# Latent attention: probabilities copied within SBUF ahead of rounded 32-bit transposes, with SyncE in source order

## The chip, the cores and the metric

The kernel runs on one core of a Trainium2 chip. The metric is the time of one execution on the device in microseconds (us). A core has TensorE (PE; its weight loads are shown as PEld), VectorE (DVE), ScalarE (ACT), GpSimd (POOL) and SyncE (SP), which here only issues transfers (DMAs). ScalarE, VectorE and TensorE meet in PSUM, the matmuls' output memory; all else lies in SBUF, the on-chip memory, or in DRAM. A time is given as the median of several runs; the profile comes from one profiled execution.

## What is computed

One decoder block with two attention mixers in parallel, for 1024 tokens of width 1024 in float32: sliding-window attention (A) and multi-head latent attention (B), gated and summed, then a gated feed-forward part. The change is in B, which has 8 heads, keys of 64 + 32 numbers and values of 64, and is causal:

```python
def one_block(args):
    qn, qr, n = args
    s = (einsum('bqhd,bkhd->bhqk', qn, k_nope) + einsum('bqhr,bkr->bhqk', qr, k_rope)) * scale
    qpos = n * BLOCK + jnp.arange(BLOCK)
    causal = kpos[None, :] <= qpos[:, None]
    s = jnp.where(causal[None, None], s, -jnp.inf)
    p = jax.nn.softmax(s, axis=-1).astype(v.dtype)
    return jnp.einsum('bhqk,bkhd->bqhd', p, v)
...
y = sigmoid(g_a) * (o_a @ w_o_swa) + sigmoid(g_b) * (o_b @ w_o_mla)
x = x + y @ w_out
h = rmsnorm(x)
x = x + (silu(h @ w_gate) * (h @ w_up)) @ w_down
```

The queries are swept in blocks of 128. Block n has n + 1 blocks of keys.

## The kernel before

**Numbers in two halves.** The matmuls take a 32-bit type that is rounded (`F32R`, "rounded 32-bit"). To keep accuracy an operand is split into a rounded part and the rest: `split` casts on ScalarE (L163) and subtracts on VectorE (L166), and `mm3` adds three products (L172 to L174). A tile of type `F32R` must be written as such; the kernel gets round this for the windowed attention by copying a float32 tile by DMA into an `F32R` tile, whose bits are then taken as they are (`norm`, the `move` entry, L1095, and `sw_pT`, L1008).

**The stage around the change.** After the projections (`prod_q`, `prod_k`, `prod_v`, `prod_rope`) comes a loop over 64 steps t, 8 heads by 8 query blocks. Within a head the blocks are taken in the order 2, 3, 6, 7, 0, 1, 4, 5 (`order`), so a step handles 3, 4, 7, 8, 1, 2, 5 or 6 blocks of keys. `scores(t)` multiplies into a score tile `scb` in PSUM (two buffers); VectorE adds the mask and takes the extreme (L1263); ScalarE takes the exponential with its row sum into `p` in SBUF (L1264); GpSimd inverts the sum (L1265) and scales `p` (L1266). `transposes(t)` turns each 128x128 block of `p` by TensorE (L1280) into PSUM tiles `pTb` of up to four blocks and splits them into `pth` and `ptl`. `pv` multiplies two query blocks by the values (L1302, L1303) three steps later.

In step t the source issues `scores(t + 2)`, then `pv`, the loads of a later head's queries and keys (`load_q`, three transfers of 768 KB in all, in the fifth step of a head; `load_k`, 512 KB, in the seventh), then two of the products of the gated output projection of A as filler (`mix_a`, tile `oA`), then `transposes(t)`. Behind these come transfers and splits for the filler and for the stage that follows: gate tiles (`load_sig`, `sg`), weights (`st.load_to`, `wr`), and `out_sums`, which adds blocks of the output weights in DRAM, by copies that SP issues (two of 1 MB at t = 34, one each at t = 47 and 54) and by accumulating transfers that GpSimd issues (t = 40, 43, 50, 58). `prod_k` for later heads runs in the first steps and stores its result to DRAM (`kn_d`, L1211); `mix_a` stores four of its tiles (`ar_d`, L1364).

**What sets the order.** Until the loop TensorE and SP follow the source by hand. In the loop they do not: a planner orders each engine's instructions by its own estimate of costs, except for those marked to keep their place. Tiles of one pool are given out as they come free: 21 shared slots of 4 KB a partition (`U`) hold `p`, `pth`, `ptl`, `sg`, `wr` and others. A transfer's issue waits on its engine until its data and its slot are ready, and what stands behind it on that engine waits too.

Of the kernel before, what the change touches and what calls it, by code (L numbers as in the profile page):

```python
# [17 lines left out]
P = 128  # L18
# [71 lines left out]
def hybrid_block_kernel(  # L90
# [39 lines left out]
    def psum_phase(name, bufs):  # L130
        if psum:
            psum.pop("cm").close()
        psum["cm"] = ExitStack()
        psum["x"] = psum["cm"].enter_context(tc.tile_pool(name=name, bufs=bufs, space=PSUM))
# [18 lines left out]
    def P1(name, shape=(P, 512), dt=F32):  # L153
        return ps1.tile(list(shape), dt, tag="ps", name=uid(name))
# [6 lines left out]
    def split(hi, lo, src, eng=None):  # L161

        i = nc.scalar.copy(hi, src)  # L163
        if held[0]:
            tc.keep_in_program_order(i)
        (eng or nc.vector).tensor_tensor(lo, src, hi.bitcast(F32), op=ALU.subtract)  # L166
# [15 lines left out]
    def blk(b, n=1):  # L182
        return slice(b * P, (b + n) * P)

    def half(s):
        return slice(512 * s, 512 * s + 512)
# [1014 lines left out]
    def prod_k(j, s):  # L1201
        ps = P1("k")
        mm3(ps, [((wk[0][:, k, blk(j)], wk[1][:, k, blk(j)]), (ckv[k][0][:, half(s)], ckv[k][1][:, half(s)]))
                 for k in range(2)])
        if j == 0:
            for u in range(2):
                split(kT[u][0:64, 0, half(s)], kT[u][0:64, 1, half(s)], ps[64 * u:64 * u + 64])
            return
        t = U("kns", F32R, (P, 2, 512))
        split(t[:, 0], t[:, 1], ps)  # L1210
        nc.sync.dma_start(kn_d[j][:, :, half(s)], t.bitcast(F32))  # L1211

    def prod_v(b):
        ps = P1("v")
        mm3(ps, [((ckv[k][0][:, blk(b)], ckv[k][1][:, blk(b)]), (wv[0][:, k], wv[1][:, k])) for k in range(2)])
        if b % 2 == 0:
            t = V("vM", F32R, (P, 2, NH, P))
            vM.extend([t[:, 0], t[:, 1]])
        split(vM[b][:, :, 0:HD], vM[b][:, :, HD:P], ps.rearrange("p (h d) -> p h d", d=HD))

    def load_k(h):
        nc.sync.dma_start(kT[h % 3][0:64].bitcast(F32), kn_d[h // 2, 64 * (h % 2):64 * (h % 2) + 64])

    def load_q(h):
        if h >= 2:
            qT[h] = V("qT", F32R, (P, 2, S))
            nc.sync.dma_start(qT[h][0:64].bitcast(F32), qn_d[h // 2, 64 * (h % 2):64 * (h % 2) + 64])
        t = qT[h]
        for i in range(2):
            nc.sync.dma_start(t[64 + 16 * i:80 + 16 * i].bitcast(F32), qr_d[i, 16 * h:16 * h + 16])  # L1230
# [11 lines left out]
    def scores(t):  # L1242
        h, n = step(t)
        w = (n + 1) * P
        sc = PX("scb", (P, 1024))
        qh, ql = (qT[h][0:QK, i] for i in range(2))
        kh, kl = (kT[h % 3][0:QK, i] for i in range(2))
        cw = 320 if w == 640 else 512
        for c0 in range(0, w, cw):
            c1 = min(c0 + cw, w)  # L1250
            kc = slice(c0, c1)
            o = slice(c0 // cw * 512, c0 // cw * 512 + c1 - c0)
            nc.tensor.matmul(sc[:, o], qh[:, blk(n)], kh[:, kc], start=True, stop=False)
            nc.tensor.matmul(sc[:, o], qh[:, blk(n)], kl[:, kc], start=False, stop=False)
            nc.tensor.matmul(sc[:, o], ql[:, blk(n)], kh[:, kc], start=False, stop=True)  # L1255
        nm = tiny("nmb")
        p = U("p")
        den = tiny("denb")
        s_, m_, p_ = sc[:, 0:w], mask[:, S - w:], p[:, 0:w]
        if cw == 320:  # L1260
            s_ = sc.rearrange("p (a c) -> p a c", a=2)[:, :, 0:320]
            m_, p_ = (v.rearrange("p (a c) -> p a c", a=2) for v in (m_, p_))
        nc.vector.tensor_tensor_reduce(s_, s_, m_, 1.0, -NEG, op0=ALU.add, op1=ALU.min, accum_out=nm)  # L1263
        nc.scalar.activation(p_, s_, AF.Exp, scale=-1.0, bias=nm, accum_out=den)  # L1264
        nc.gpsimd.tensor_tensor(den, den, neg_one[:, 0:1], op=ALU.pow)  # L1265
        nc.gpsimd.tensor_scalar(p[:, 0:w], p[:, 0:w], den, 0.0, op0=ALU.mult, op1=ALU.add)  # L1266
        live[t] = p

    def transposes(t):
        h, n = step(t)  # L1270
        p = live.pop(t)
        j, odd = divmod(n, 2)
        if not odd:
            pts[(h, j)] = [(U("pth", F32R, (P, 4, 256)), U("ptl", F32R, (P, 4, 256)))
                           for _ in range((2 * j + 5) // 4)]
        for k0 in range(0, n + 1, 4):
            m = min(4, n + 1 - k0)
            pp = P1("pTb", (P, 4, P))
            for i in range(m):
                nc.tensor.transpose(pp[:, i], p[:, blk(k0 + i)], ident)  # L1280
            hi, lo = pts[(h, j)][k0 // 4]
            split(hi[:, 0:m, blk(odd)], lo[:, 0:m, blk(odd)], pp[:, 0:m])

    def pv(h, j):
        tiles = pts.pop((h, j))
# [57 lines left out]
    def mix_a(dc, sh, c0, n, ps=None):  # L1343
        if ps is not None:
            oa_ps[(dc, sh)] = ps
        ps = oa_ps[(dc, sh)]
        if (sh, c0) == (0, 0):
            if dc >= 4:
                ar[dc] = gate[dc]
            elif dc % 2 == 0:  # L1350
                t = V("ar", F32, (P, 2, S))
                ar[dc], ar[dc + 1] = t[:, 0], t[:, 1]
            if dc % 2 == 0:
                wo[dc // 2] = st.get(("oa", dc // 2))
        w = wo[dc // 2]
        mm3(ps, [((w[0][:, c, blk(dc % 2)], w[1][:, c, blk(dc % 2)]), oaT[(c, sh)]) for c in range(c0, c0 + n)],
            c0 == 0, c0 + n == 4)
        if c0 + n == 4:
            nc.vector.scalar_tensor_tensor(ar[dc][:, half(sh)], gate[dc][:, half(sh)], 1.0, oa_ps.pop((dc, sh)),
                                           op0=ALU.add, op1=ALU.mult)  # L1360
            if sh == 1:
                gate.pop(dc)
                if dc >= 4:
                    nc.sync.dma_start(ar_d[dc - 4], ar.pop(dc))  # L1364

    obT = {}

# [41 lines left out]
    prod_q(3, 0)  # L1409
    prod_q(3, 1)  # L1410
    psum_phase("psb", 2)
    prod_v(4)
    scores(0)
    prod_k(1, 0)
# [1 line left out]
    scores(1)  # L1416
    prod_v(5)
    prod_v(6)
    prod_v(7)
    load_k(2)  # L1420
    first = {0: (2, 0), 1: (2, 1), 2: (3, 0), 3: (3, 1)}
    fill = {}
# [4 lines left out]
    w_at = {t: u[0] // 2 for t, u in fill.items() if u[0] % 2 == 0 and u[1:] == (0, 0)}  # L1427
    g_at = {a: fill[b][0] for a, b in zip([3] + slots, slots) if fill[b][1:] == (0, 0)}
    g_at[NT - 3] = 3
    pvq = []  # L1430
    OUT_AT = {34: 0, 40: 1, 43: 2, 47: 3, 50: 4, 54: 5, 58: 6}
    for t in range(NT):
        h, n = divmod(t, NB)
        if t + 2 < NT:
            scores(t + 2)
        while pvq and pvq[0][0] <= t:
            pv(*pvq.pop(0)[1:])
        if n == 4 and h + 2 < NH:
            load_q(h + 2)
        if n == 6 and h + 3 < NH:  # L1440
            load_k(h + 3)
        hh, nn = step(t)
        if nn % 2 == 1:
            pvq.append((t + 3, hh, nn // 2))
        e = t - (NT - 8)
        if e == 6:
            psum_phase("psc", 4)
        if t in first:
            prod_k(*first[t])
        if t in fill:  # L1450
            dc, sh, c0 = fill[t]
            mix_a(dc, sh, c0, 2, P1("oA") if c0 == 0 else None)
        if t == NT - 1:
            mix_a(13 // 2 ^ 4, 13 % 2, 0, 4, PX("oA"))
        transposes(t)
        if t in OUT_AT:
            out_sums(OUT_AT[t])
        held[0] = True
        if t in g_at:
            load_sig(g_at[t])  # L1460
        if t in fill and fill[t][1:] == (0, 0):
            twice_sigmoid(gate[fill[t][0]])
        if t == NT - 1:
            twice_sigmoid(gate[3])
        if t == 3:
            load_oa(0, 1)
            load_oa(1, 1)
        if t < 4 or 6 <= t < 10:
            split_oa(t % 4 // 2 if t < 4 else (t - 6) // 2, t // 6, t % 2)
        if t + 6 in w_at or t == 0:  # L1470
            st.load_to(st.index[("oa", w_at.get(t + 6, 2))])
        if t + 2 in w_at:
            st.conv_to(st.index[("oa", w_at[t + 2])])
        if e == 4:
            load_sigs(DCS[0])
        if -3 <= e < 3:
            split_ob((e + 3) // 2, (e + 3) % 2)
        if e in (2, 6):
            st.load_to(st.index[("ob", 0 if e == 2 else 2)])
        if e == 6:  # L1480
            st.conv_to(st.index[("ob", 0)])
        held[0] = False
    rest = [(i // 2 ^ 4, i % 2) for i in range(14, 16)]
    mix_a(*rest.pop(0), 0, 4, PX("oA"))
    for _, hp, j in pvq:
# [626 lines left out]
```

## Time and profile before

| | |
|---|---|
| median of 3 runs | 1323.54 us (1322.53 to 1324.08) |
| span of the profiled execution | 1323.3 us |
| busy: PE, DVE, ACT, POOL | 99%, 69%, 48%, 42% of the span |
| granted TensorE clock | 0.999 of full speed |
| DMA | 245.12 MB, mean 185 GB/s |
| transposes of the latent attention, first to last start | 386.0 to 553.1 us |

A row of the groups names the line of the code, the engine, the operation, and the tiles as out<-in; then count, and durations in ns. A row of the timeline gives start and duration in us, then the same names, and in brackets the idle time before it with what ended it. A row of the waits says who waited for whom, with the total in us, the times and the longest. A row of the transfers gives the tiles, the issuing queue (SPq, POOLq), the count, the size of one and the median time from issue to landing. Successive matmuls overlap in their records, so their price is the distance of their starts.

### The profile page before, as it was taken

Reading aid. Unit: us, or ns where it says so; the run is one execution under the profiler, and the core shown is the slowest. Engines: PE = TensorE matmul, PEld = TensorE weight load, DVE = VectorE, ACT = ScalarE, POOL = GpSimd, SP = SyncE. Lnnn points to the kernel's source line nnn. Section 1 sums busy time; section 2 is a strip of 40 time slices with the busy share of each in tenths; the row PEclk is TensorE's granted clock in tenths of the full one; section 3 lists DMA queues with packets and bytes.
Section 4 is the critical chain, followed back from the end, with each engine's and each line's share of the span. In section 5 each row is a group of like instructions: output and inputs, shape, how many; then the busy total and the mean of one; then the engine's idle time right before and its main releaser. Section 6 shows DMA issues by size and latency. Waiting matters only on the chain.

```text
span 1323.3 us, 19060 instructions
## 1 busy us (share of the span) xinstructions
PE 1310.9 (99%) x6516; PEld 1103.7 (83%) x6516; DVE 917.0 (69%) x1517; ACT 634.6 (48%) x1282; POOL 559.0 (42%) x619
## 2 busy tenths in 40 slices
PE   9999999999999999999999999999999999999997
PEld 6899888888888889888888888888888888888886
DVE  6868787786767777777779655656666554664863
ACT  7444667665557666755355232323222223644452
POOL 1116545653324556312232465777567631022521
PEclk9999999999999999999999999999999999999999
DMA  9464344456577477898531334655544435996504
GB/s 359 167 195 154 125 162 145 140 184 212 166 241 201 97 223 160 277 322 195 181 122 48 112 130 172 235 195 206 183 181 148 150 112 198 378 376 224 175 17 142
DMA packets 92192, 245.12 MB, mean 185 GB/s; under 512 B 10304, under 2 KB 17984, under 8 KB 90944
## 3 DMA queue, kind: packets, MB, share of 16 engines
q1 hardware_dynamic: 87264, 233.15, 50.9%
q0 software_dynamic: 3392, 8.39, 3.6%
q10 hardware_dynamic: 1440, 2.36, 0.5%
q8 instruction: 52, 0.85, 0.3%
q14 instruction: 44, 0.36, 0.1%
HBM read 161.16 MB, written 78.51 MB: 181 GB/s over the span
## 4 chain that ended last, share of the span: by engine, by line
PE 63%; DVE 2%; issue 1%; POOL 1%; ACT 1%; POOLq 0%; DVEq 0%; ACTq 0%
PE fa L174 6%; PE fa L172 6%; PE fa L173 6%; PE fd L173 5%; PE fd L172 5%; PE fd L174 5%; PE fb L173 5%; PE fb L174 5%; PE fb L172 5%; PE xo L174 2%; PE xo L172 2%; PE xo L173 2%; PE pTb L1280 1%; PE oB L174 1%; PE oB L172 1%
## 5 line engine op out<-in xcount | busy, mean ns | idle before, releaser
L166 DVE TENSOR_TENSOR wl<-wr,wl 128x512 fp32r<-128x512 f32 x150 | 142.5, 973 | 74.7 <-ACT wl L163 74.2
L166 DVE TENSOR_TENSOR lrv<-lr,lrv 128x1024 fp32r<-128x1024 f32 x77 | 105.5, 1401 | 48.2 <-ACT lrv L163 45.6
L163 ACT CAST lrv<-lr 128x1024 fp32r<-128x1024 f32 x77 | 80.2, 1054 | 90.4 <-PE fd L174 56.7
L172 PE MATMUL fd<-lrv 128*128 128x512 f32 x308 | 119.8, 389 | 0.0
L173 PE MATMUL fd<-lrv 128*128 128x512 f32 x308 | 119.8, 389 | 0.0
L174 PE MATMUL fd<-lrv 128*128 128x512 f32 x308 | 119.8, 389 | 0.0
L177 POOL TENSOR_TENSOR wr<-wr,sm 128x512 f32<-128x512 f32 (+1 forms) x38 | 45.5, 1208 | 139.9 <-DVE wl L166 121.7
L163 ACT CAST wl<-wr 128x512 fp32r<-128x512 f32 x150 | 86.7, 621 | 4.8 <-DVE t3l L177 2.8
L166 DVE TENSOR_TENSOR wl<-sm,wl 128x512 fp32r<-128x512 f32 x60 | 50.2, 859 | 42.1 <-ACT wl L163 41.9
L1265 POOL TENSOR_TENSOR denb<-denb,neg_one 128x1 f32<-128x1 f32 x64 | 39.8, 622 | 92.7 <-ACT p L1264 80.7
L172 PEld LDWEIGHTS fd<-lrv 128*128 128x128 f32 x308 | 57.8, 188 | 12.1
L174 PEld LDWEIGHTS fd<-lrv 128*128 128x128 f32 x308 | 57.8, 188 | 12.0
L173 PEld LDWEIGHTS fd<-lrv 128*128 128x128 f32 x308 | 57.8, 188 | 11.9
L1264 ACT ACTIVATE p<-scb,nmb 128x384 f32<-128x384 f32 (+3 forms) x64 | 47.7, 746 | 32.0 <-DVE nmb L1263 23.5
L361 POOL TENSOR_SCALAR ms<-ss 128x1 f32<-128x1 f32 x32 | 8.9, 278 | 125.9 <-ACT xn L1742 47.5
L1263 DVE CUSTOM_DVE_ANT_0 scb<-scb,mask 128x384 f32<-128x384 f32 (+3 forms) x64 | 48.5, 761 | 17.2 <-PE scb L1255 14.6
L1638 ACT ACTIVATE act<-sm 128x512 f32<-128x512 f32 x11 | 7.0, 635 | 102.1 <-DVE sm L180 102.1
L166 DVE TENSOR_TENSOR ptl<-pTb,pth 128x512 fp32r<-128x512 f32 (+2 forms) x96 | 50.0, 550 | 7.9 <-ACT pth L163 7.7
L163 ACT CAST pth<-pTb 128x512 fp32r<-128x512 f32 (+2 forms) x96 | 43.4, 480 | 18.1 <-PE pTb L1280 17.1
L1266 POOL TENSOR_SCALAR p<-p,denb 128x384 f32<-128x384 f32 (+3 forms) x64 | 48.2, 753 | 6.3
L172 PE MATMUL fa<-t1h,wl 128*128 128x512 f32 x120 | 47.1, 392 | 0.4 <-ACT wl L163 0.4
L172 PE MATMUL fb<-t2h,wl 128*128 128x512 f32 x120 | 47.1, 392 | 0.0
(357 smaller groups left out, 4260.7 us busy)
## 6 DMA issues: line engine op xcount, KB each, us to landing
lr<-la_d SPq DMA_DIRECT2D x77, 256.0 KB, 5.4
wr<-in_w_gate_dram SPq DMA_DIRECT2D x22, 512.0 KB, 4.3
wr<-in_w_up_dram SPq DMA_DIRECT2D x22, 512.0 KB, 5.0
la_d<-sd SPq DMA_DIRECT2D x22, 512.0 KB, 5.2
wd<-in_w_down_dram SPq DMA_DIRECT2D x22, 512.0 KB, 6.6
rb_d<-wd SPq DMA_DIRECT2D x22, 512.0 KB, 2.7
lr<-rb_d SPq DMA_DIRECT2D x44, 256.0 KB, 5.4
lr<-in_w_down_dram SPq DMA_DIRECT2D x33, 256.0 KB, 5.4
```

Source lines behind the costliest of these rows:

```text
L163: i = nc.scalar.copy(hi, src)
L166: (eng or nc.vector).tensor_tensor(lo, src, hi.bitcast(F32), op=ALU.subtract)
L172: nc.tensor.matmul(ps, ah, bh, start=first and i == 0, stop=False, skip_group_check=go_on)
L173: nc.tensor.matmul(ps, ah, bl, start=False, stop=False, skip_group_check=go_on)
L174: nc.tensor.matmul(ps, al, bh, start=False, stop=last and i == n - 1, skip_group_check=go_on)
L177: eng.tensor_tensor(out, a, b, op=ALU.subtract)
L361: nc.gpsimd.tensor_scalar(ms, ss, 1.0 / width, EPS, op0=ALU.mult, op1=ALU.add)
L1263: nc.vector.tensor_tensor_reduce(s_, s_, m_, 1.0, -NEG, op0=ALU.add, op1=ALU.min, accum_out=nm)
L1264: nc.scalar.activation(p_, s_, AF.Exp, scale=-1.0, bias=nm, accum_out=den)
L1265: nc.gpsimd.tensor_tensor(den, den, neg_one[:, 0:1], op=ALU.pow)
L1266: nc.gpsimd.tensor_scalar(p[:, 0:w], p[:, 0:w], den, 0.0, op0=ALU.mult, op1=ALU.add)
L1280: nc.tensor.transpose(pp[:, i], p[:, blk(k0 + i)], ident)
```

## The change

It has five parts. (1) `scores` no longer hands `p` to the transposes: `move()` allocates a tile `pr` of rounded type and has SP copy the used columns of `p` into it; one is issued in each step behind `transposes(t)`, and two before the loop, for which `scores(2)` moves ahead of the loop. (2) The transposes read `pr`, with the rounded identity, into a PSUM tile of rounded type, which is read back as float32. (3) In the loop the scores run three steps ahead (`AHEAD = 3`) and not two. (4) The stores of `kn_d` and `ar_d` are put into a list, `later`, and issued by `stores()` once a step, after `scores` and `pv`. (5) From `prod_v(4)` to the end of the loop SP follows the source's order; in it `load_q` and `load_k` come behind the transposes and the copy.

```diff
--- before.py
+++ after.py
@@ -1208,7 +1208,7 @@
             return
         t = U("kns", F32R, (P, 2, 512))
         split(t[:, 0], t[:, 1], ps)
-        nc.sync.dma_start(kn_d[j][:, :, half(s)], t.bitcast(F32))
+        later.append((kn_d[j][:, :, half(s)], t.bitcast(F32)))
 
     def prod_v(b):
         ps = P1("v")
@@ -1264,7 +1264,19 @@
         nc.scalar.activation(p_, s_, AF.Exp, scale=-1.0, bias=nm, accum_out=den)
         nc.gpsimd.tensor_tensor(den, den, neg_one[:, 0:1], op=ALU.pow)
         nc.gpsimd.tensor_scalar(p[:, 0:w], p[:, 0:w], den, 0.0, op0=ALU.mult, op1=ALU.add)
-        live[t] = p
+        moves.append((t, p, w))
+
+    moves = []
+    later = []
+
+    def move():
+        t, p, w = moves.pop(0)
+        live[t] = U("pr", F32R)
+        nc.sync.dma_start(live[t].bitcast(F32)[:, 0:w], p[:, 0:w])
+
+    def stores():
+        while later:
+            nc.sync.dma_start(*later.pop(0))
 
     def transposes(t):
         h, n = step(t)
@@ -1275,11 +1287,11 @@
                            for _ in range((2 * j + 5) // 4)]
         for k0 in range(0, n + 1, 4):
             m = min(4, n + 1 - k0)
-            pp = P1("pTb", (P, 4, P))
+            pp = P1("pTb", (P, 4, P), F32R)
             for i in range(m):
-                nc.tensor.transpose(pp[:, i], p[:, blk(k0 + i)], ident)
+                nc.tensor.transpose(pp[:, i], p[:, blk(k0 + i)], ident_r)
             hi, lo = pts[(h, j)][k0 // 4]
-            split(hi[:, 0:m, blk(odd)], lo[:, 0:m, blk(odd)], pp[:, 0:m])
+            split(hi[:, 0:m, blk(odd)], lo[:, 0:m, blk(odd)], pp.bitcast(F32)[:, 0:m])
 
     def pv(h, j):
         tiles = pts.pop((h, j))
@@ -1361,7 +1373,7 @@
             if sh == 1:
                 gate.pop(dc)
                 if dc >= 4:
-                    nc.sync.dma_start(ar_d[dc - 4], ar.pop(dc))
+                    later.append((ar_d[dc - 4], ar.pop(dc)))
 
     obT = {}
 
@@ -1409,6 +1421,8 @@
     prod_q(3, 0)
     prod_q(3, 1)
     psum_phase("psb", 2)
+    sp_order = tc.manual_schedule(engines={engines.SP})
+    sp_order.__enter__()
     prod_v(4)
     scores(0)
     prod_k(1, 0)
@@ -1416,7 +1430,11 @@
     scores(1)
     prod_v(5)
     prod_v(6)
+    move()
+    stores()
+    scores(2)
     prod_v(7)
+    move()
     load_k(2)
     first = {0: (2, 0), 1: (2, 1), 2: (3, 0), 3: (3, 1)}
     fill = {}
@@ -1427,18 +1445,16 @@
     w_at = {t: u[0] // 2 for t, u in fill.items() if u[0] % 2 == 0 and u[1:] == (0, 0)}
     g_at = {a: fill[b][0] for a, b in zip([3] + slots, slots) if fill[b][1:] == (0, 0)}
     g_at[NT - 3] = 3
+    AHEAD = 3
     pvq = []
     OUT_AT = {34: 0, 40: 1, 43: 2, 47: 3, 50: 4, 54: 5, 58: 6}
     for t in range(NT):
         h, n = divmod(t, NB)
-        if t + 2 < NT:
-            scores(t + 2)
+        if t + AHEAD < NT:
+            scores(t + AHEAD)
         while pvq and pvq[0][0] <= t:
             pv(*pvq.pop(0)[1:])
-        if n == 4 and h + 2 < NH:
-            load_q(h + 2)
-        if n == 6 and h + 3 < NH:
-            load_k(h + 3)
+        stores()
         hh, nn = step(t)
         if nn % 2 == 1:
             pvq.append((t + 3, hh, nn // 2))
@@ -1453,6 +1469,12 @@
         if t == NT - 1:
             mix_a(13 // 2 ^ 4, 13 % 2, 0, 4, PX("oA"))
         transposes(t)
+        if moves:
+            move()
+        if n == 4 and h + 2 < NH:
+            load_q(h + 2)
+        if n == 6 and h + 3 < NH:
+            load_k(h + 3)
         if t in OUT_AT:
             out_sums(OUT_AT[t])
         held[0] = True
@@ -1480,6 +1502,8 @@
         if e == 6:
             st.conv_to(st.index[("ob", 0)])
         held[0] = False
+    stores()
+    sp_order.__exit__(None, None, None)
     rest = [(i // 2 ^ 4, i % 2) for i in range(14, 16)]
     mix_a(*rest.pop(0), 0, 4, PX("oA"))
     for _, hp, j in pvq:
```

## The prediction

> **What bounds the kernel now.** I read the page's totals first, then the busy time of the stage that the change touches (its first and last transposes date it: 386 to 553 us), then what ends the waits there.
>
> ```profile
> span 1323.3 us, 19060 instructions
> PE 1310.9 (99%) x6516; PEld 1103.7 (83%) x6516; DVE 917.0 (69%) x1517; ACT 634.6 (48%) x1282; POOL 559.0 (42%) x619
> ```
>
> ```profile
> 386.00:554.00 168.00, 165.05 (x1059) 144.93 (x1058) 129.60 (x271) 118.90 (x266) 88.64 (x128) 1.00 0.67 182
> 554.00:600.00 46.00, 46.00 (x212) 38.38 (x211) 34.06 (x50) 24.23 (x31) 7.06 (x8) 1.00 0.99 329
> ```
>
> The columns after the window are its length, busy PE, PEld, DVE, ACT and POOL, the granted clock, the DMA engines' share and GB/s. TensorE is busy in 165.05 of the stage's 168 us and in all 46 us behind it, at full clock, so a TensorE microsecond saved here reaches the end if nothing new makes it wait. The next engine, VectorE, is at 77% in the stage. The DMA engines stand at 0.67.
>
> ```profile
> PEld scb L1253 <- ACT p L1264: 1.7, 5, 0.5
> ...
> PEld pTb L1280 <- POOL p L1266: 0.8, 1, 0.8
> ```
>
> These are TensorE's two longest waits for the softmax in the stage, the score products' for a score tile that the exponential still reads and the transposes' for the scaled probabilities: 2.5 us (the columns are total, times, longest).
>
> **The transposes.** The change makes the 288 transposes of the probabilities 32-bit rounded. The form has rows already: the windowed attention transposes such tiles at L1008.
>
> ```profile
> L1280 PEld LDWEIGHTS pTb<-ident_r,p x288: 137/140/145, 385.8 to 553.0; 128*128 128x128 f32 x144
> L1280 PE MATMUL pTb<-ident_r,p x288: 270/272/328, 386.0 to 553.1; 128*128 128x128 f32 x144
> ```
>
> ```profile
> L1008 PEld LDWEIGHTS pT<-ident_r,per x120: 137/139/143, 152.7 to 316.3; 128*128 128x128 f32 x120
> L1008 PE MATMUL pT<-ident_r,per x120: 222/247/253, 152.9 to 316.4; 128*128 128x128 f32 x120
> ```
>
> The durations (272 and 247 ns) overlap from one instruction to the next, so the price is the distance of starts. First the plain form, then the rounded one, both in TensorE's order of time:
>
> ```profile
> 479.00 0.93 PE L1280 MATMUL pTb<-ident_r,p 128*128 128x128 f32 x7
> 479.68 0.36 PE L1253 MATMUL scb<-kT,qT 96*128 96x256 f32 x1
> 479.88 0.28 PE L1254 MATMUL scb<-kT,qT 96*128 96x256 f32 x1
> 480.00 0.28 PE L1255 MATMUL scb<-kT,qT 96*128 96x256 f32 x1
> ```
>
> ```profile
> 175.22 0.80 PE L1008 MATMUL pT<-ident_r,per 128*128 128x128 f32 x8
> 175.85 0.33 PE L948 MATMUL qT<-ident_r,qn 128*128 128x128 f32 x2
> 176.02 0.47 PE L172 MATMUL fb<-t3h,wl 128*128 128x512 f32 x1
> 176.33 0.40 PE L173 MATMUL fb<-t3l,wl 128*128 128x512 f32 x1
> 176.56 0.40 PE L174 MATMUL fb<-t3h,wl 128*128 128x512 f32 x1
> ```
>
> A 256-column product normally takes 0.12 (479.88 to 480.00), so the seven plain transposes hold the array until 479.88 - 0.12 = 479.76: 0.76 us, 0.109 each. In the second list a 512-column product takes 0.23, so the ten rounded ones hold it until 176.10: 0.88 us, 0.088 each; inside the group they stand (175.85 - 175.22)/8 = 0.079 apart, and 176.10 - 176.02 = 0.08 follows the group as a bubble. A group of n therefore costs 0.079n + 0.08 against 0.109n. A head has 36 blocks in eight groups (1 to 8 blocks): 36 x 0.030 - 8 x 0.08 = 0.44 us a head, 3.5 us in eight heads. If neighbouring groups run together, it is 288 x 0.021 = 6.0; with no bubble at all, 288 x 0.030 = 8.6. I take 4.5, between the first two, since the groups here are as mixed as in the row of ten. The evacuations (cast on ScalarE, subtraction on VectorE) keep their shapes and counts.
>
> [...]
>
> **The copy.** In its place comes, for each of the 64 steps, one transfer within SBUF of the tile's used columns (64 KB for each of 1 to 8 blocks). It stands between GpSimd's scaling (L1266) and the transposes, so its latency lies on the path of every step. In exchange the scores are issued three steps ahead and not two. What a step has now:
>
> ```profile
> 435.92 1.12 POOL L1266 TENSOR_SCALAR p<-p,denb 128x1024 f32<-128x1024 f32 x1
> ...
> 437.65 0.37 POOL L1266 TENSOR_SCALAR p<-p,denb 128x128 f32<-128x128 f32 x1
> ...
> 442.96 0.48 POOL L1266 TENSOR_SCALAR p<-p,denb 128x256 f32<-128x256 f32 x1
> ```
>
> ```profile
> 438.38 1.04 PE L1280 MATMUL pTb<-ident_r,p 128*128 128x128 f32 x8
> 441.03 0.30 PE L1280 MATMUL pTb<-ident_r,p 128*128 128x128 f32 x1
> 444.12 0.38 PE L1280 MATMUL pTb<-ident_r,p 128*128 128x128 f32 x2
> ```
>
> From the end of the scaling to the first transpose lie 438.38 - 437.04 = 1.3 us (8 blocks), 3.0 (1 block) and 0.7 (2 blocks), 1.7 on the mean. A step lasts (553.1 - 386.0)/63 = 2.65 us, by the first and last starts of the transposes quoted above. One step more ahead makes the room 4.3 us on the mean, 4.0 for the 512 KB tile, 3.3 for the 128 KB one. The copy's price:
>
> ```profile
> per<-pe SPq DMA_DIRECT2D x14, 512.0 KB, 3.2
> ...
> lat_d<-lat SPq DMA_DIRECT2D x8, 128.0 KB, 1.7
> ```
>
> The windowed attention's copy of 512 KB within SBUF lands 3.2 us after issue; the nearest small transfer, to DRAM, takes 1.7. Both fit into their rooms, by 0.8 and 1.6 us, as long as nothing is ahead of them on the queue. So I cost the copies at nothing where the queue is free. The cover is the extra step; without it each step would be late by some 3.2 - 1.7 = 1.5 us.
>
> The queue is not always free.
>
> ```profile
> q1 hardware_dynamic: 5840, 26.14, 53.2%
> ...
> sg<-gate_d SPq DMA_DIRECT2D x12, 512.0 KB, 5.1
> ```
>
> ```profile
> DMA  0000000000000000989999889999899699999989
> ```
>
> ```profile
> qT<-qn_d SPq DMA_DIRECT2D x1, 512.0 KB, 12.5
> qT<-qr_d SPq DMA_DIRECT2D x2, 128.0 KB, 12.2
> wt_d<-in_w_out_dram SPq DMA_DIRECT2D x2, 9.4
> ```
>
> The first two are of the stage, 386 to 554 us. The slices are of 203 to 206.3 us, when a 512 KB copy ran: it fills the engines from slice 17 to about 32, some 1.3 us. All copies are 288 x 64 KB = 18.9 MB, 36 of these, so about 47 us of full engines: 28% of the stage on top of 67%, 0.95 together. The last three rows are of the issues between 464 and 470 us: the two weight copies within DRAM (`out_sums(0)`) landed after 9.4 us, and a load issued behind them on the same queue after 12.5. In the new order they come right after a copy at t = 34, and the next copy is issued one step (2.65 us) later, behind them: it lands about 9.4 - 2.65 = 6.8 us after its issue, 2.5 over the mean room of 4.3. That is one stall of up to 2.5 us; the two 1 MB copies (t = 47 and 54) are half as long and come out within the room. The other loads (`load_q`, 768 KB; `load_k`, `load_sig`, weights, 512 KB each) now follow a copy and have a step's time to drain. Smaller stalls of other copies I take as none likeliest. Bounds of this term: 0, and 12 us (first rival); taken, 2.0.
>
> **SyncE's order.** SP now follows the source through the stage, so each instruction that waits holds the next copy. Before:
>
> ```profile
> SPq L1364 <- DVE sg L1359: 32.3, 4, 14.9
> ```
>
> The stores of L1364 waited up to 14.9 us for VectorE; the change puts them and the stores of the keys into a list that is issued at the start of a following step, when VectorE is done, so they cost nothing there. `load_k` (L1222) waits for the scores that still read its buffer; with `load_q` it moves behind the transposes and the copy of its step, and the scores of its buffer's old head have by then been issued two steps or more before. Its landing has 15 steps until use, `load_q` nine, so a later issue is free. A load that waits for one of the 21 shared tile slots would hold a copy; each step now holds about two tiles more. I cost that at nothing; without a free slot it would be a step's delay, 2.65 us at a time. GpSimd's queue keeps its order; its accumulating transfers wait for SP's weight copies, which the new order issues at their own step and not earlier, with three steps (8 us) to spare.
>
> **The waits for the softmax.** Of the 2.5 us, the transposes' 0.8 go when the scores run a step ahead; those of `scb` stay, as the score tiles still have two buffers. Bounds -2.5 and 0; taken -1.0, nearest to the transposes' row.
>
> **The sum.** 1323.3 - 4.5 - 1.0 + 2.0 = 1319.8 us. The profiled execution's span, 1323.3, lies 0.24 below the median of the runs (1323.54), so I carry the number over as it is. About 0.2%, 2.6 us, is what a measurement of this kernel can tell from no change.
>
> **The rivals.** *Late copies (slower).* If copies meet loads on the queue, they land like `sg`, after 5.1 us, and not like `per`. It decides from a landing of 4.3 us on: at 5.1 a copy is 0.8 late, and with the 128 KB tile's room of 3.3 us 1.8; I take 1.1, nearer to the mean. TensorE takes its instructions in order, so scores behind the late transposes are late too and nothing catches up. For the eleven `load_q` and `load_k` steps that is 12 us: 1323.3 - 4.5 + 12 = 1331. For it speaks 0.95 of DMA time; against it, that loads follow a copy and not the other way round. [...] Chance 0.28.
>
> *Even.* The copies lose about what the transposes win, by a few late ones: -4.5 + 4 gives 1323. For it: the rooms are only 0.8 us larger than a landing for the largest tiles. Chance 0.20.
>
> *The rounded transposes are no faster here.* The weight loads take 140 and 139 ns in both forms; if these set the distance in the short groups of this stage, the first term goes and the rest stays: 1323.3 - 1.0 + 2.0 = 1324.3. [...] Chance 0.04.
>
> *All of it.* No copy is late, the bubbles fall into waits, and the softmax's waits go: -6.0 - 2.5 gives 1314.8. Chance 0.10.
>
> **How the numbers follow.** The forecast (1317.5 to 1320.6) has 0.38. Faster: 0.38 + 0.10 = 0.48. Same: 0.20 + 0.04 = 0.24. Slower: 0.28. The range 1314.5 to 1330 leaves out half of the late copies (0.14) and a little of the best case (0.05); the faster cases alone, which hold 0.48, reach from 1314 to 1320.6.
>
> **What would show it.** In the profile after: the rounded transposes some 0.08 apart in a group; the scaling's end to the transposes some 4 us; the copies' median landing under 4 us; TensorE's waits in the stage for the copies about 2 us in total, most of it beside `out_sums`. If the copies' landing is above 4.3 us, or TensorE is busy under 163 of 168 us, the forecast is wrong and the first rival holds. If the stage gets shorter and the end does not, I misread what bounds the stage behind it.

## The result and the profile after

The changed kernel takes 1361.4 us (median of 4 runs, 1359.32 to 1368.17) against 1323.76 of before (4 runs, 1322.53 to 1324.08): a ratio of 1.030, 95% interval 1.027 to 1.032. It is 38 us slower. The profiled execution of after has a span of 1357.4 us, 34.1 over that of before.

The totals of its page:

```profile
span 1357.4 us, 19220 instructions
PE 1320.7 (97%) x6516; PEld 1113.3 (82%) x6516; DVE 919.7 (68%) x1517; ACT 633.5 (47%) x1282; POOL 554.3 (41%) x619
...
PEclk9999999999998898999999999999999999999999
```

TensorE has the same 6516 products, and its share falls from 99 to 97%. New is the third row: the granted clock, which was full throughout, drops in slices 12, 13 and 15 (407 to 475 and 509 to 543 us), inside the stage of the change. The stage's window of before, in after (length; busy PE, PEld, DVE, ACT, POOL; clock; DMA share; GB/s), and a second one that holds the whole stage:

```profile
386.00:554.00 168.00, 146.61 (x864) 128.37 (x863) 104.33 (x217) 94.36 (x213) 69.68 (x106) 0.88 0.80 231
384.00:590.00 206.00, 178.84 (x1061) 155.28 (x1061) 130.60 (x270) 118.33 (x264) 85.26 (x127) 0.90 0.80 236
```

The whole stage of before, in the same view:

```profile
386.00:557.00 171.00, 168.05 (x1077) 147.57 (x1076) 131.11 (x273) 119.90 (x266) 88.64 (x128) 1.00 0.68 186
```

About the same work takes 206 us and not 171. TensorE stands idle for 206 - 178.84 = 27.2 us, where it was 171 - 168.05 = 3.0: 24 us more. And it runs at 0.90 of its clock, which costs up to 0.10 x 206 = 21 us. Together that is 45, and the stage is only 35 longer, since the rounded transposes are cheaper and 16 of 1077 products lie outside the window. So there are two losses of similar size, and the next views say where they begin. The rows of the transposes and of the copies (the last is a line of its own in the view of the tile `pr`):

```profile
L1292 PE MATMUL pTb<-ident_r,pr x288: 221/248/342, 384.3 to 588.3; 128*128 128x128 f32 x144
```

```profile
L1275 SPq DMA_DIRECT2D pr<-p x64: 464/467/812, 378.6 to 581.2; - x64
...
DMA to landing us min/median/max: 1.8/4.6/9.8
```

The median copy lands 4.6 us after its issue; the prediction put the limit at 4.3. What ended the waits in the stage, first on all engines, then on SP's queue:

```profile
PE pTb L1292 <- DMA pr<-p: 21.4, 12, 3.5
...
PEld scb L1253 <- ACT p L1264: 2.4, 5, 0.8
```

```profile
SPq L1275 <- POOL p L1266: 74.7, 43, 5.5
...
SPq L1279 <- DVE sg L1371: 5.0, 2, 2.6
```

TensorE waits 21.4 us for copies, in twelve stalls; in before the longest wait for the scaled probabilities was 0.8 us. SP is not what makes the copies late: it mostly stands ready at the copy's line and waits for GpSimd's scaling (74.7 us). In the trace of after the median copy is issued 0.03 us behind the end of its scaling, the most delayed one 3.1 us behind it. The stores of the list held it up for 5.0 us in two places. The time goes between issue and landing. The issues of the whole stage, by size:

```profile
pr<-p SPq DMA_DIRECT2D x8, 512.0 KB, 2.9
pr<-p SPq DMA_DIRECT2D x8, 448.0 KB, 4.2
kT<-kn_d SPq DMA_DIRECT2D x6, 512.0 KB, 9.0
...
pr<-p SPq DMA_DIRECT2D x8, 384.0 KB, 6.8
...
pr<-p SPq DMA_DIRECT2D x7, 256.0 KB, 7.0
...
pr<-p SPq DMA_DIRECT2D x7, 192.0 KB, 7.5
...
pr<-p SPq DMA_DIRECT2D x8, 64.0 KB, 2.1
```

The largest copies land in 2.9 us, smaller ones in 7. So it isn't their size; it is what was issued just ahead of them. Within a head, `load_q` follows the copy of five blocks and `load_k` that of three, and the copies of 6, 3 and 4 blocks (384, 192, 256 KB) are the next three. One head's SP queue, start and duration of the issues, and the landing times of the same transfers:

```profile
426.45 0.47 SPq L1275 DMA_DIRECT2D pr<-p  x1
426.97 0.59 SPq L1227 DMA_DIRECT2D qT<-qn_d  x1
427.61 1.06 SPq L1230 DMA_DIRECT2D qT<-qr_d  x2
428.77 1.60 SPq L1275 DMA_DIRECT2D pr<-p  x2
430.43 0.60 SPq L1222 DMA_DIRECT2D kT<-kn_d  x1
432.36 0.47 SPq L1275 DMA_DIRECT2D pr<-p  x1
```

```profile
qT<-qn_d SPq DMA_DIRECT2D x1, 512.0 KB, 5.2
kT<-kn_d SPq DMA_DIRECT2D x1, 512.0 KB, 8.5
...
pr<-p SPq DMA_DIRECT2D x1, 384.0 KB, 6.5
pr<-p SPq DMA_DIRECT2D x1, 320.0 KB, 2.4
qT<-qr_d SPq DMA_DIRECT2D x2, 128.0 KB, 5.8
pr<-p SPq DMA_DIRECT2D x1, 256.0 KB, 7.0
pr<-p SPq DMA_DIRECT2D x1, 192.0 KB, 6.3
```

Issue plus landing gives the order: the copy of five blocks 428.9 (426.45 + 2.4), `load_q`'s large part 432.2, its two small ones 433.3 and 434.1, the copy of six blocks 435.3 (428.77 + 6.5), that of three 436.2, `load_k` 438.9, the copy of four blocks 439.4. All of them land in order of issue. The trace also has every packet that the DMA engines moved. The packets of `load_q` are on the engines from 428.4 to 432.8, 3.7 us of all 16 engines by the sum of their times, and those of `load_k` from 434.2 to 438.0, 2.4 us. The copy of six blocks is issued 1.8 us after `load_q`'s first issue, and its own first packet starts at 431.4. TensorE meanwhile:

```profile
435.37 0.68 PE L1292 MATMUL pTb<-ident_r,pr 128*128 128x128 f32 x6 [1.25 <-DMA pr<-p]
435.88 0.46 PE L1255 MATMUL scb<-kT,qT 96*128 96x512 f32 x1
```

It starts the six transposes at 435.37, just as the copy has landed, after an idle 1.25 us; the score product behind them in its order waits as well. From the copy's issue to its transposes it is 6.6 us, where the prediction's room was 4.3. What follows, in the windows' view:

```profile
434.00:437.40 3.40, 2.15 (x19) 1.96 (x18) 2.74 (x6) 1.97 (x4) 1.58 (x2) 1.00 1.06 245
437.40:444.20 6.80, 5.98 (x23) 5.29 (x23) 2.46 (x9) 2.23 (x6) 2.55 (x4) 0.50 0.69 244
444.20:447.60 3.40, 3.40 (x25) 3.09 (x24) 2.14 (x4) 2.02 (x6) 1.03 (x2) 1.00 0.56 174
```

The stall is inside the first window, in which TensorE is busy for 2.15 of 3.4 us. In the two windows' length behind it the granted clock is 0.50, although TensorE has work for 5.98 of 6.8 us; then it is full again. There are six such stretches in the stage, 41 us together, and none in before.

### The profile page after: what moved, and what is told of

Read it like the earlier page. It is cut to its first block, busy times and chain, and to the rows that moved or that the text cites. A ratio compares the mean times of both kernels' runs of the same rounds, so it can differ in the third digit from the quotient of the medians.

```text
span 1357.4 us, 19220 instructions
## 1 busy us (share of the span) xinstructions
PE 1320.7 (97%) x6516; PEld 1113.3 (82%) x6516; DVE 919.7 (68%) x1517; ACT 633.5 (47%) x1282; POOL 554.3 (41%) x619
## 4 chain that ended last, share of the span: by engine, by line
PE 82%; issue 7%; POOL 5%; DMA 4%; DVE 2%; SPq 0%; POOLq 0%; ACT 0%; ACTq 0%; DVEq 0%
PE fa L172 8%; PE fa L174 8%; PE fa L173 8%; PE fb L172 6%; PE fb L173 6%; PE fb L174 6%; PE fd L172 5%; PE fd L173 5%; PE fd L174 5%; DMA pr<-p 2%; POOL p L1266 2%; PE xo L174 2%; PE xo L172 2%; PE xo L173 2%; POOL denb L1265 2%
## 5 line engine op out<-in xcount | busy, mean ns | idle before, releaser
L1292 PE MATMUL pTb<-ident_r,pr 128*128 128x128 f32 x288 | 36.1, 255 | 23.3 <-DMA pr<-p 21.4
L1292 PEld LDWEIGHTS pTb<-ident_r,pr 128*128 128x128 f32 x288 | 32.1, 147 | 31.4 <-issue 13.9
```

What stands on the lines that cost most here:

```text
L1292: nc.tensor.transpose(pp[:, i], p[:, blk(k0 + i)], ident_r)
```

## The experiments

Three theories stood after the result. *Engine time*: the copies wait because the loads and weight copies occupy the 16 DMA engines. *Place in the queue*: they wait because they stand behind loads on SP's queue. *The rest of the change*: the third step, SP's order or the transposes lose the time. The kernel before ran beside each set, at medians of 1322.5 to 1323.5.

**Without the loads.** The edit of after:

```diff
     def load_k(h):
-        nc.sync.dma_start(kT[h % 3][0:64].bitcast(F32), kn_d[h // 2, 64 * (h % 2):64 * (h % 2) + 64])
+        if h == 2:
+            nc.sync.dma_start(kT[h % 3][0:64].bitcast(F32), kn_d[h // 2, 64 * (h % 2):64 * (h % 2) + 64])
...
     def load_q(h):
...
-            qT[h] = V("qT", F32R, (P, 2, S))
-            nc.sync.dma_start(qT[h][0:64].bitcast(F32), qn_d[h // 2, 64 * (h % 2):64 * (h % 2) + 64])
+            qT[h] = qT[h - 2]
+            return
```

> The changed kernel without the loads of later heads' queries and keys (load_q from head 2 on, load_k from head 3 on; these heads read an earlier head's tiles, so part of the computation is changed). Queue theory (copies are late because loads stand ahead of them on SyncE's queue): the copies' median landing falls from 4.6 to about 3 us, the half-clock stretches in the stage shrink from six to two or fewer (those at the two 1 MB weight copies may stay), and the time to about 1330 us. Bandwidth theory (the DMA engines are full whatever stands where): 7 of some 49 MB go, so the stage gains about a seventh of its 38 us: 1355 us.

Measured: 1350.13 us, ratio 1.021 (1.019 to 1.023), so 11 us of the 38 come back. It lies between the two theories' numbers, and five stretches of half clock are left, 20.5 us in place of 41, where the queue theory asked for two or fewer. Steps 12 to 30 settle more than the total: in e1 only copies, gate tiles, filler weights and a few stores are on the queue there. From the first transposes of step 12 to those of step 31, in e1, in before and in after:

```profile
424.00:473.00 49.00, 48.29 (x320) 42.23 (x318) 34.21 (x77) 31.95 (x74) 25.90 (x40) 1.00 0.42 154
```

```profile
419.70:469.50 49.80, 49.09 (x318) 43.32 (x317) 34.52 (x77) 32.33 (x76) 26.24 (x40) 1.00 0.54 138
```

```profile
424.70:485.10 60.40, 55.37 (x326) 48.96 (x324) 36.67 (x79) 32.23 (x76) 25.84 (x40) 0.89 0.68 188
```

Without loads these nineteen steps take 49.0 us and are shorter than before (49.8); with loads they take 60.4. Here the copy is free once the loads are gone. The 11.4 us between e1 and after can be told apart. In this stretch of after, TensorE waits for three copies, each of them the six blocks behind a `load_q`:

```profile
PE pTb L1292 <- DMA pr<-p: 4.2, 3, 1.5
```

Two of these waits are followed by 6.8 us at half clock, which costs up to half of these 13.7 us, 6.8: with the waits, up to 11.0. The remaining loss of e1 lies in other steps, where the stores of the keys or `out_sums` are in flight. TensorE's waits for copies in the whole stage of e1:

```profile
PE pTb L1293 <- DMA pr<-p: 14.8, 8, 3.5
```

**The loads on another queue.** ScalarE issues them, the three of `load_q` in the same way as that of `load_k`, so the copies no longer stand behind them on SP's queue:

```diff
-        nc.sync.dma_start(kT[h % 3][0:64].bitcast(F32), kn_d[h // 2, 64 * (h % 2):64 * (h % 2) + 64])
+        nc.scalar.dma_start(kT[h % 3][0:64].bitcast(F32), kn_d[h // 2, 64 * (h % 2):64 * (h % 2) + 64])
```

> The changed kernel with load_q (from head 2 on) and load_k issued by ScalarE, on its own queue, all bytes kept. Queue theory: a copy no longer stands behind a load, so its median landing falls to about 3.5 us and the time to about 1335 us. Bandwidth theory: the engines serve both queues by turns, the copies stay at 4.6 us and the time at 1360 us. If ScalarE itself is held by a wait of such a load, its casts come late and the time rises above 1361 us.

Measured: 1373.77 us, ratio 1.039 (1.037 to 1.041), 12 us worse than after. Its copies:

```profile
DMA to landing us min/median/max: 1.8/4.7/10.8
```

At the median they land no sooner, 4.7 against 4.6. By size they change places:

```profile
pr<-p SPq DMA_DIRECT2D x8, 320.0 KB, 5.8
...
pr<-p SPq DMA_DIRECT2D x7, 192.0 KB, 5.1
```

The copy of three blocks, which stood behind `load_k`, lands after 5.1 us and not 7.5; that of five, ahead of `load_q`, after 5.8 and not 3.6. So the place on the queue bears on which copies are late, but not on how late they are at the median. In the loop ScalarE's order is the planner's, so the loads also leave at other times. Its trace has 55 us at half clock in the stage and not 41, worth up to 7 of the 12 us.

**The copy on GpSimd's queue** is the other way round:

```diff
-        nc.sync.dma_start(live[t].bitcast(F32)[:, 0:w], p[:, 0:w])
+        nc.gpsimd.dma_start(live[t].bitcast(F32)[:, 0:w], p[:, 0:w])
```

> The changed kernel with the 64 copies issued by GpSimd, on its own queue, right behind its scaling; the loads stay with SyncE. Queue theory: copies no longer stand behind the loads, but GpSimd spends about 0.9 us on each issue (the duration of its other transfers' issues) beside 1.35 us of its own work in a step of 2.65, so about 1340 us, with half-clock stretches mainly beside the accumulating transfers on the same queue. Bandwidth theory: 1360 us.

Measured: 1402.35 us, ratio 1.061 (1.059 to 1.064); TensorE's waits for the copies rise to 55.2 us, and their median landing is 4.9 us.

```profile
PE pTb L1292 <- DMA pr<-p: 55.2, 17, 8.3
```

Both speak against the place in the queue as the cause, e2 more plainly: in e3 GpSimd also spends its own time on the issues, some 0.6 us each in its timeline (0.598 at the median).

**Rounding without a copy.** Before, with one edit: GpSimd's scaling writes the rounded tile, and the transposes read that.

```diff
-        nc.gpsimd.tensor_scalar(p[:, 0:w], p[:, 0:w], den, 0.0, op0=ALU.mult, op1=ALU.add)
-        live[t] = p
+        r = U("pr", F32R)
+        nc.gpsimd.tensor_scalar(r[:, 0:w], p[:, 0:w], den, 0.0, op0=ALU.mult, op1=ALU.add)
+        live[t] = r
```

(and the rounded identity and PSUM tile, as in the change)

> The kernel before with one part of the change alone: GpSimd's scaling writes a rounded 32-bit tile and the transposes read that, in their rounded form; no copy, scores two steps ahead, SyncE's order left to the planner. The scaled probabilities are rounded at GpSimd, so what the split keeps of their low bits is changed. My first term (0.109 to about 0.093 us a transpose): 1323.7 - 4.5 = 1319 us. Rival (the form does not matter in these short groups): 1323.7 us.

Measured: 1319.24 us (8 runs), ratio 0.997 (0.996 to 0.998), 4.2 us under before. The first term of the sum is so confirmed by itself; the stage's own share of it follows further below, beside e9.

**The change without its copy.** After, with the same edit of GpSimd's scaling (`p` in `move` is then the rounded tile); SP's order, the third step, the list of stores and the place of the loads stay:

```diff
-        live[t] = U("pr", F32R)
-        nc.sync.dma_start(live[t].bitcast(F32)[:, 0:w], p[:, 0:w])
+        live[t] = p
```

> The changed kernel without the copy alone: GpSimd writes its scaled probabilities into the rounded 32-bit tile itself (so their low bits are rounded away there) and the transposes read that; SyncE's order, the three steps ahead, the deferred stores and the place of the loads stay as in the change. Theory that the copy's time under other transfers is the whole loss: 1318 us, as the copyless e4 (1319.2) or a little better by the third step. Rival (the fixed order of SyncE, or the planner's new order of TensorE with three steps ahead, carries part of the loss): above 1330 us.

Measured: 1323.59 us (11 runs), ratio 1.000 (0.999 to 1.001). The copy alone costs 1361.4 - 1323.6 = 38 us, the whole loss. The theory's 1318 is missed all the same: what is left of the change besides the transposes costs 1323.6 - 1319.2 = 4.4 us (4.2 by the ratios).

**Neither loads nor `out_sums`.** As e1, and the weight copies of `out_sums` are gone as well:

```diff
-        if t in OUT_AT:
-            out_sums(OUT_AT[t])
```

> The changed kernel without its other large transfers in the loop: no load_q from head 2 and no load_k from head 3 (earlier heads' tiles are read) and no out_sums (the stage behind reads blocks of the output weights in place of their sums), so part of the computation is changed; the 64 copies stay. Theory of engine time (a copy is late when another transfer is in flight): median landing about 2.6 us, late copies only in the first ten steps and at the end, no half clock between steps 12 and 56, time about 1333 us. Rival (the copy's bare latency is too long for the room): 1350 us as in e1.

Measured: 1330.57 us, ratio 1.006 (1.004 to 1.007): 31 of the 38 us come back, about what engine time asks.

```profile
DMA to landing us min/median/max: 1.9/2.7/8.3
```

```profile
PE pTb L1293 <- DMA pr<-p: 3.7, 3, 1.6
```

With the engines quiet the median copy lands in 2.7 us, and TensorE's waits for copies fall from 21.4 to 3.7 us. **Without `out_sums` alone** (the loads stay):

> The changed kernel without out_sums alone (the stage behind reads blocks of the output weights in place of their sums, so part of the computation is changed); all loads of queries and keys stay. Without both it took 1330.6 (e6), without the loads alone 1350.1 (e1). If the two shares add up, the sums are worth 1350.1 - 1330.6 = 19.5 us: 1342 us. If each hides the other (a copy late behind one would have been late behind the other), it stays above 1350 us.

Measured: 1349.52 us, ratio 1.019 (1.017 to 1.021). Each of the two alone returns 11 to 12 us, both together 31: the effects do not add. That part of either one's stalls falls on time that the other has lost already would explain it, but no run shows it.

**A fourth step ahead:**

```diff
+    scores(3)
+    move()
-    AHEAD = 3
+    AHEAD = 4
```

> The changed kernel with the scores four steps ahead and not three (one more copy before the loop); nothing else. Theory that the room of 4.3 us is what the copies overrun: the room becomes about 7 us, copies that land after 4.6 us at the median are in time and only those above 7 (about one in four) are late: 1340 us. Rival (the delays feed back through TensorE's order and the slots, so more distance does not help): 1358 us or more.

Measured: 1363.01 us, ratio 1.030 (1.028 to 1.032): no gain. The copies' median goes up with it, and the waits hardly down:

```profile
DMA to landing us min/median/max: 1.8/5.4/12.1
```

```profile
PE pTb L1292 <- DMA pr<-p: 17.1, 9, 3.9
```

The expectation that more room hides the copies is refuted. Why it doesn't is open.

**Plain transposes with the copy.** After with `pr`, PSUM tile and identity as plain float32:

```diff
-        live[t] = U("pr", F32R)
+        live[t] = U("pr")
-                nc.tensor.transpose(pp[:, i], p[:, blk(k0 + i)], ident_r)
+                nc.tensor.transpose(pp[:, i], p[:, blk(k0 + i)], ident)
```

> The changed kernel with plain 32-bit transposes of the copied tile; copy, order and distance stay. Theory that TensorE waits for copies anyway: part of the dearer transposes (288 x 0.021 = 6 us) falls into waits, 1361.4 + 3 = 1364 us. Rival (the transposes stand on the path in full): 1367 us or more.

Measured: 1357.69 us, ratio 1.027 (1.025 to 1.029), 3.7 us under after and not above it: the dearer transposes cost nothing here, and both numbers expected are missed. The reason given for the first, that they would fall into waits, is not what the trace shows: TensorE waits for copies as long as in after (21.7 us, in 13 stalls). What differs is the clock, 0.95 and not 0.90 in the same window:

```profile
384.00:590.00 206.00, 179.54 (x1074) 155.38 (x1074) 132.24 (x272) 119.54 (x266) 85.83 (x128) 0.95 0.81 241
```

Its trace has 20.5 us at half clock and not 41, worth up to 10 us. Why the clock drops less often is open.

**The third step ahead alone.** e4 with the scores three steps ahead, nothing else:

```diff
+    scores(2)
-        if t + 2 < NT:
-            scores(t + 2)
+        if t + 3 < NT:
+            scores(t + 3)
```

> e4 (the kernel before, GpSimd writing the rounded tile that the transposes read, no copy) with the scores three steps ahead. Theory that the 4.3 us between e4 (1319.2) and e5 (1323.6) come from SyncE's fixed order and the later loads: 1318 to 1319.5 us. Rival (three steps ahead cost them, by the planner's other order of TensorE): 1323 us.

Measured: 1323.75 us (11 runs), ratio 1.001 (1.000 to 1.002), 4.5 us over e4. That is the whole rest that e5 left, so it is the third step and not SP's order. The stage starts 2.5 to 3.5 us earlier in the profiled execution of e4 than in the others, so the windows here run from event to event, from the first product of the tile `v` to the last one of the filler, in before, e4 and e9:

```profile
356.30:560.30 204.00, 201.05 (x1226) 175.12 (x1225) 148.03 (x301) 134.41 (x294) 94.06 (x135) 1.00 0.69 197
```

```profile
352.80:553.00 200.20, 196.48 (x1226) 170.93 (x1225) 147.72 (x301) 134.79 (x294) 94.53 (x135) 1.00 0.69 198
```

```profile
355.30:559.40 204.10, 198.71 (x1227) 171.45 (x1226) 147.18 (x301) 134.56 (x294) 92.78 (x135) 1.00 0.66 192
```

The same products take 3.8 us less in e4 than before, which is the transposes' share. In e9 all of it is lost again: TensorE is idle for 5.4 and not 3.7 us and busy for 2.2 us more.

**After with SP left to the planner:**

```diff
-    sp_order = tc.manual_schedule(engines={engines.SP})
-    sp_order.__enter__()
```

> The changed kernel with SyncE's order left to the planner as before; copy, distance and the source's order of issue stay. Theory of engine time: the same bytes meet the same copies, so 1361 us, within 8 either way. Rival (the fixed order puts the loads ahead of the copies): the planner places the copies better and it is under 1345 us.

Measured: 1364.65 us, ratio 1.031 (1.029 to 1.032). SP's order is neutral.

**One half of the probabilities.** e4, and the lower half is left out, as the tile that is transposed has been written as a rounded one:

```diff
-            split(hi[:, 0:m, blk(odd)], lo[:, 0:m, blk(odd)], pp.bitcast(F32)[:, 0:m])
+            nc.scalar.copy(hi[:, 0:m, blk(odd)], pp.bitcast(F32)[:, 0:m])
...
-            nc.tensor.matmul(po[:, q_off:], vst, lo[:, kb % 4, q_off:], start=False, stop=kb == nk - 1)
```

> e4 (GpSimd writes the rounded tile, no copy, two steps ahead) without the low half of the probabilities: the 96 subtractions on VectorE and the 160 products of the low half with the values are left out. If GpSimd's write has rounded the tile already, the low half holds nothing and only time goes: 128 x 0.12 + 32 x 0.06 = 17 us of TensorE, 1319.2 - 17 = 1302 us. Rival (TensorE then waits for the softmax, whose chain is unchanged, and the stage does not shrink by all of it): 1310 us.

Measured: 1306.4 us (4 runs), ratio 0.987 (0.985 to 0.989): faster than both kernels, between the two numbers expected. What now shows among TensorE's waits is the softmax (rows below), and the trace has 6.8 us at half clock in the stage, where e4 has none; that is worth up to 3.4 of the 4.4 us that are missing to 1302.

```profile
PEld scb L1253 <- ACT p L1264: 3.5, 5, 1.8
...
PE scb L1253 <- ACT p L1264: 2.3, 3, 1.6
```

## Why the prediction was wrong

The direction was the first rival's, at three times its price. The forecast's sum failed in one step above all, the price of the copies: +2.0 was taken, and 38 us were measured.

- **The rounded transposes, -4.5: right.** e4 measures -4.2 by the medians, -3.7 by the ratio, -3.8 in the stage. In the list above, six of them and their bubble take 435.88 - 435.37 = 0.51 us; the prediction's formula gave 0.079 x 6 + 0.08 = 0.55.
- **The copies, +2.0: wrong, the failed step.** It said that the loads "now follow a copy and have a step's time to drain", and took other late copies as none. In the list of one head they do not: `load_q` holds the engines for 3.7 us and `load_k` for 2.4, and the next copies are issued 1.8 and 1.9 us behind them, not 2.65. So not one copy is late: 35 of the 64 land more than 4.3 us after their issue, by the medians of the sizes three in each head, and others around `out_sums` and the stores of the keys. The room was sized right: in e9, three steps ahead and without a copy, 4.4 us lie on the mean between the scaling's end and the transposes. It was compared with 3.2, the landing of a copy in the windowed attention; in e6, where the engines are quiet, copies of that size land in 2.9 (six of them, issued between 415 and 540 us), so the price is right for an empty queue and useless for a full one. The share of 0.95 that I worked out was a warning of this: after has 0.80 in a stage 35 us longer. As a mean it does not show the bursts.
- **The rival "late copies", +12: the right mechanism, the wrong size.** It counted eleven steps of 1.1 us. TensorE's waits for copies are 21.4 us in twelve stalls, 1.8 each, up to 3.5; its whole additional idle time is 24 us. That eleven and twelve are so close is chance, for they are not the same steps: the copies behind `load_k` land late but, in steps 12 to 30, are not waited for, and about half of the stalls stand beside the stores of the keys and `out_sums`. The other half of the loss, the halved clock behind the stalls, up to 21 us, stood in none of the cases, so the range could not hold the result.
- **The queue.** The prediction let a copy land behind what stands ahead of it on SP's queue. The landings in order of issue, 428.9 to 439.4 us in the list of one head, agree with it. But it made the place on the queue look like the cause, and e2 and e3 show that another queue does not remove the lateness (4.7 and 4.9 us at the median, against 4.6); in e2 it shifts to other copies.
- **The waits for the softmax, -1.0: wrong sign.** The third step costs 4.4 to 4.5 us by itself (e5, e9). The score tiles' waits stayed, as foreseen (2.4 us in after). The transposes' wait is gone: in e9 each scaling ends at least 2.1 us ahead of its transposes. But the same products take TensorE longer in the order that the planner makes with three steps.
- **SP's order, 0: right.** e10 and the pair e5 and e9 put it within a few us of nothing.
- **The signs named** for a failure both came: a landing over 4.3 us (4.6), and TensorE busy under 163 of 168 us (146.6).

Shown by experiment: that the copy is the whole loss (e5), that it is late from what other transfers occupy (e6 against e2 and e3: 2.7 us at the median against 4.7 and 4.9), that distance, SP's order and the transposes are not the cause (e7, e10, and e4 and e8). Worked out from the traces: the halved clock's share of the loss. No run changes it by itself, but it comes and goes with the late copies: the stage has 41 us of it in after, 31 in e11, 20 in e1, 3.4 in e6 and none in before, e4 and e9 (e5 and e12, which have no copy, have 3.4 and 6.8). Open: what part of the 12 us that the loads on ScalarE's queue cost is the clock, why a fourth step doesn't help, why plain transposes lose less clock, which of the planner's moves makes the third step dear, and in e12, whether GpSimd's write rounds away all of the lower half, which no profile shows.

## What to carry over

Before a transfer is put on a path that every step walks, add up how long the stage's other transfers hold the DMA engines and in which bursts they are issued, and take its price from a row under such a load; here another queue did not get it past them on the whole (a median landing of 4.7 us in e2 against 4.6). On an engine that is as full as TensorE here (busy for 168.05 of 171 us before), a stall may cost more than its length: behind the one of 1.25 us the granted clock was 0.50 for 6.8 us. Where a tile is wanted in another type of the same width, look first whether the engine that writes it last can write that type: this gave the transposes' gain here without any copy (4.2 us in e4).

## What the hardware showed beyond this

- **The granted clock was 0.50 behind windows that were only partly idle.** The six stretches of 0.50 last 3.4 to 10.2 us, all multiples of 3.4 us, and stand on one grid of that length. TensorE was busy for 0.10 to 0.63 of the grid window ahead of each. The busy share alone does not settle it: the next row, of a window with 1.98 of 3.4 us (0.58), has full clock behind it, and so has the window from 580.8 to 584.2 with 1.7 (0.50).

```profile
481.80:485.20 3.40, 1.98 (x11) 1.33 (x9) 2.73 (x5) 0.00 (x0) 0.00 (x0) 1.00 0.99 359
485.20:488.60 3.40, 2.42 (x16) 1.95 (x16) 2.03 (x4) 2.96 (x6) 1.20 (x2) 1.00 1.05 275
```

  The window from 434.0 to 437.4, with more work in it than either of these (2.15 us, 0.63), has 6.8 us of 0.50 behind it. What else decides it is open.
- **512 KB did not always take the same time.** In the stage of after, the packets of 8 KB that load queries and keys to 64 partitions take 0.62 us each at the median, those of 4 KB on the same queue, of transfers over 128 partitions (the largest copies within SBUF, weights, gates, stores), 0.16. For 512 KB that is 64 x 0.62 / 16 = 2.5 us of all 16 engines against 128 x 0.16 / 16 = 1.3: the loads of this stage cost about twice what their bytes suggest.
